# A two-layer attention kernel on one core: the stick-breaking scan as a running product, with a part of the splitting moved to GpSimd

## The chip, the core and the metric

The kernel runs on one core of a Trainium2 chip. The metric is the device time of one execution in microseconds (us). Three executions of the kernel before took 2713.68, 2715.38 and 2715.46 us; the median is 2715.38 us. One more execution was profiled.

## What is computed

The program is two layers for 2048 tokens of 1024 features, in float32. Layer 0 is a gated linear attention; the change does not touch it. Layer 1 is stick-breaking attention with 16 heads of 64 features:

```python
z = einsum('bhtd,bhsd->bhts', q_block, k) * scale
strictly_before = s_idx < t_idx
log_beta = log_sigmoid(z)
log_one_minus = where(strictly_before, log_beta - z, 0.0)
log_survive = cumsum(log_one_minus, axis=3, reverse=True) - log_one_minus
weights = where(strictly_before, exp(log_beta + log_survive), 0.0)
o = einsum('bhts,bhsd->bhtd', weights, v)
out = (o * silu(g)) @ w_out
```

A key s has beta = sigmoid(z); its weight is beta times the product of (1 - beta) of all keys between it and the query. Around it stand a modulated norm ahead and the output projection and a last norm behind.

## The kernel before, in words

**Layout.** Features lie on the partitions. A float32 operand of a large product is held as hi + lo, both float32r, and three products are accumulated (`mm3`, L150 to L152). The tokens come in 4 groups of 512 (g), layer 1's heads in 8 pairs (p).

**Layer 1.** For each pair and group, `pair_linear` makes keys, values, queries and gate of the group (L734 to L799). A `Unit` is a head (h) and a group of queries (g) against one group of keys (c); for a head it goes from c = g, the diagonal, down to c = 0. A unit has four tiles of 128 queries (tb), each 128x512, on the diagonal 128, 256, 384 and 512 wide. The work of a tile:

- `scores` (L815): two products make z in a bank of the pool `pz`, which has two banks (L821, L822). ScalarE makes S = sigmoid(z) in SBUF (L825) and 1 - beta = sigmoid(-z) in the bank itself (L826). On the diagonal GpSimd masks 128 columns of S (L828). VectorE scans from the last key back: S[s] = (1 - beta[s]) S[s + 1] + beta[s] (L830), started with 0 on the diagonal, elsewhere with the first column of the tile of the unit before. The bank is free when the scan is done.
- `turn` (L834): for 128 keys (sb), up to four transposes of S tiles into a bank pt of the pool `pw`, of two banks (L838); ScalarE copies it as sh (hi, L841), VectorE makes sl = pt - sh (lo, L842).
- `values` (L845): two products of sh and sl with the differences of neighbouring values v (L854, L855), summed in the bank o. After the last, `finish` adds the halves (L867, L868) and multiplies by the gate.

```python
        steps = [(u, j) for u in units for j in range(4)]
        for i, (u, j) in enumerate(steps):
            u.scores(j)
            turns.append((u, j))
            step(fill, (i + 0.7) / len(steps))
            if len(values) > LAG_V: ...   # values of an earlier tile
            step(fill, (i + 1) / len(steps))
            if len(turns) > LAG_T: ...    # turn of the tile five steps back
```

**What sets the order.** TensorE's order is the order of the program text: the loop above (L978 to L995). A group has 8 (g + 1) steps. Between the steps runs the fill: the 33 parts of `pair_linear` of the next group (three products each), and in groups 2 and 3 the weights of the next pair (`load_scaled`: splits L132, L133 and weighted sums L138, L140). In layer 1 the orders of ScalarE, VectorE, GpSimd and of the DMA queue on SP are made by a scheduler at build time and are then fixed: each engine takes its instructions in that order and waits by semaphores. `S`, `sh`, `sl` and others are tiles of one pool of 22 buffers (`m2`).

## Time and profile before

| | |
|---|---|
| median of three runs | 2715.38 us |
| profiled execution, first to last instruction | 2716.1 us |
| TensorE busy, matmuls | 2622.9 us (97%) |
| VectorE busy | 2112.2 us (78%) |
| ScalarE busy | 1785.9 us (66%) |
| GpSimd busy | 131.7 us (5%) |
| scans L830, 384 off the diagonal | 490.1 us |
| sl, L842, 640 | 381.3 us |
| second sigmoid L826, 640 | 344.4 us |

The profiled execution's own time is its span, 2716.1 us, 0.7 us over the median of the runs; the profile gives no other time around it. Layer 0 ends near 975 us, the attention of layer 1 runs from there to about 2600 us, and the last projection ends the program. The profile has the engines as PE (TensorE), PEld (its weight loads), ACT (ScalarE), DVE (VectorE), POOL (GpSimd) and SP. Matmuls overlap in the pipeline, so a busy PE is not one at its peak; the start-to-start distance of matmuls tells its pace.

### The profile page before, as it was taken

What the parts mean: (1) busy time and instruction counts of PE and PEld (TensorE: products, weight loads), DVE (VectorE), ACT (ScalarE), POOL (GpSimd) and SP (SyncE); (2) the same over time, 40 slices, a digit from 0 to 9 for tenths busy, and PEclk for the clock granted to TensorE, in tenths of its full rate; (3) what the DMA queues carried; (4) which work ended last, traced back from release to release, by engine and by line L of the source; (5) the groups of instructions that cost most, each with busy time, mean ns of one, the idle gap of its engine ahead of it and who ended that gap; (6) DMA issues with size and microseconds to landing.
All of it is one profiled execution on the core that took longest, in us unless ns stands there. A gap on an engine that the chain in (4) does not pass through costs nothing.

```text
span 2716.1 us, 38447 instructions
## 1 busy us (share of the span) xinstructions
PE 2622.9 (97%) x14040; PEld 2190.1 (81%) x14040; DVE 2112.2 (78%) x2933; ACT 1785.9 (66%) x3317; POOL 131.7 (5%) x358
## 2 busy tenths in 40 slices
PE   5999999999999999999999999999999999999998
PEld 4888888888788878788787887887887887877887
DVE  7657767676675658978979969979879789789866
ACT  4746756574584457767857857767768677677744
POOL 3000000000000010000000000000000000000000
PEclk7999999999999999999999999999999999999999
DMA  6326445545631563342343334243243243323464
GB/s 246 116 76 211 150 150 179 166 142 176 225 140 63 178 238 119 105 144 89 104 138 124 108 109 152 83 143 110 75 148 109 73 149 113 115 92 114 147 214 147
DMA packets 116685, 371.93 MB, mean 137 GB/s; under 512 B 13872, under 2 KB 18096, under 8 KB 116496
## 3 DMA queue, kind: packets, MB, share of 16 engines
q1 hardware_dynamic: 116496, 369.47, 40.8%
q8 instruction: 111, 1.82, 0.3%
q14 instruction: 78, 0.64, 0.1%
HBM read 311.75 MB, written 40.89 MB: 130 GB/s over the span
## 4 chain that ended last, share of the span: by engine, by line
PE 72%; DVE 17%; ACT 5%; DMA 3%; issue 3%; SPq 0%; POOL 0%; DVEq 0%; POOLq 0%
PE pt L838 6%; DVE S L830 5%; PE z L821 4%; PE z L822 3%; PE o L855 3%; PE o L854 3%; DVE sl L842 2%; PE pg L150 2%; PE pf L150 2%; PE pf L151 2%; PE pf L152 2%; PE pg L152 2%; PE pg L151 2%; PE lv L150 2%; PE pv L444 2%
## 5 line engine op out<-in xcount | busy, mean ns | idle before, releaser
L841 ACT ACTIVATE sh<-pt 128x512 fp32r<-128x512 f32 (+3 forms) x640 | 341.0, 533 | 318.1 <-PE pt L838 305.7
L830 DVE TENSOR_TENSOR_SCAN S<-z,S,S 128x512 f32<-128x512 f32 x384 | 490.1, 1276 | 33.0 <-ACT z L826 30.8
L842 DVE TENSOR_TENSOR sl<-pt,sh 128x512 fp32r<-128x512 f32 (+3 forms) x640 | 381.3, 596 | 141.1 <-ACT sh L841 137.6
L825 ACT ACTIVATE S<-z 128x512 f32<-128x512 f32 (+3 forms) x640 | 340.1, 531 | 24.4 <-PE z L822 12.3
L838 PE MATMUL pt<-ident,S 128*128 128x128 f32 x2176 | 343.3, 273 | 2.4 <-DVE sl L842 2.4
L826 ACT ACTIVATE z<-z 128x512 f32<-128x512 f32 (+3 forms) x640 | 344.4, 538 | 0.0
L838 PEld LDWEIGHTS pt<-ident,S 128*128 128x128 f32 x2176 | 270.3, 140 | 68.7 <-issue 2.7
L821 PE MATMUL z<-k,q 128*128 128x512 f32 (+3 forms) x640 | 287.2, 449 | 32.6 <-DVE S L830 30.2
L830 DVE TENSOR_TENSOR_SCAN S<-z,S 128x128 f32<-128x128 f32 (+3 forms) x256 | 209.5, 819 | 34.3 <-ACT z L826 24.2
L822 PE MATMUL z<-k,ql 128*128 128x512 f32 (+3 forms) x640 | 234.7, 367 | 0.9 <-DMA ql<-ql 0.9
L855 PE MATMUL o<-sl,v 128*128 128x512 f32 (+3 forms) x640 | 234.0, 366 | 0.0
L854 PE MATMUL o<-sh,v 128*128 128x512 f32 (+3 forms) x640 | 231.3, 361 | 0.6
L821 PEld LDWEIGHTS z<-k,q 128*128 128x128 f32 x640 | 121.4, 190 | 63.0 <-DVE S L830 56.2
L444 PE MATMUL pv<-wh_v,h 128*128 128x256 f32 x512 | 155.6, 304 | 0.0
L445 PE MATMUL pv<-wl_v,h 128*128 128x256 f32 x512 | 145.6, 284 | 0.0
L446 PE MATMUL pv<-wh_v,h 128*128 128x256 f32 x512 | 145.6, 284 | 0.0
L854 PEld LDWEIGHTS o<-sh,v 128*128 128x128 f32 x640 | 120.5, 188 | 30.2 <-DVE oB L868 3.7
L828 POOL TENSOR_SCALAR_AFFINE_SELECT S<-S 128x128 f32<-128x128 f32 x256 | 81.9, 320 | 1295.2 <-ACT S L825 1174.8
L855 PEld LDWEIGHTS o<-sl,v 128*128 128x128 f32 x640 | 120.5, 188 | 25.3
L822 PEld LDWEIGHTS z<-k,ql 128*128 128x128 f32 x640 | 123.1, 192 | 1.2 <-issue 1.0
L150 PE MATMUL pg<-h,wh_g 128*128 128x512 f32 x256 | 112.6, 440 | 0.0
L150 PE MATMUL lk<-xb,wh_w_kv 128*128 128x512 f32 x256 | 102.0, 398 | 5.2 <-DVE oB L868 5.2
(267 smaller groups left out, 6420.3 us busy)
## 6 DMA issues: line engine op xcount, KB each, us to landing
xb<-xn SPq DMA_DIRECT2D x256, 512.0 KB, 4.9
wa_l<-in_w_ada_dram SPq DMA_DIRECT2D x40, 512.0 KB, 6.0
wr_f<-in_w_out_dram SPq DMA_DIRECT2D x40, 512.0 KB, 4.0
x<-in_x_dram SPq DMA_DIRECT2D x32, 512.0 KB, 6.4
wr_v<-in_w_v_dram SPq DMA_DIRECT2D x32, 512.0 KB, 4.6
wr_kq<-in_w_kq_dram SPq DMA_DIRECT2D x32, 512.0 KB, 4.0
wr_g<-in_w_g_dram SPq DMA_DIRECT2D x32, 512.0 KB, 3.8
wr_out<-in_w_out_dram SPq DMA_DIRECT2D x32, 512.0 KB, 3.8
```

Of the source, the lines that this page charges most:

```text
L150: nc.tensor.matmul(out, hi, x[kt][0], start=first and i == 0, stop=False)
L444: nc.tensor.matmul(o, xh, hi, start=i == 0, stop=False)
L821: nc.tensor.matmul(z, L.q[:, h, tcol], k[:, h, 0:w], start=True, stop=False)
L822: nc.tensor.matmul(z, L.ql[h][:, tcol], k[:, h, 0:w], start=False, stop=True)
L825: nc.scalar.activation(s, z, AF.Sigmoid, scale=SCALE_B)
L826: nc.scalar.activation(z, z, AF.Sigmoid, scale=-SCALE_B)
L830: nc.vector.tensor_tensor_scan(s[:, ::-1], z[:, ::-1], s[:, ::-1], 0.0 if diag else self.before.S[tb][:, 0:1], ALU.mult, ALU.add)
L838: nc.tensor.transpose(pt[:, tb * P:(tb + 1) * P], self.S[tb][:, sb * P:(sb + 1) * P], ident)
L841: nc.scalar.activation(hi, pt[:, t0 * P:], AF.Copy)
L842: nc.vector.tensor_tensor(lo, pt[:, t0 * P:], hi.bitcast(F32), op=ALU.subtract)
L854: nc.tensor.matmul(o, v, hi, start=self.diag and sb == 0, stop=False)
L855: nc.tensor.matmul(o, v, lo, start=False, stop=self.c == 0 and sb == 3)
```

## The change

S is replaced by its complement, the running product of 1 - beta, so that one sigmoid is enough, and the transposed tile is brought back by -1 (which makes -S; the differences of the values change sign too).

- Off the diagonal one sigmoid, sigmoid(-z), is written into the bank; the scan reads the bank and a column of ones broadcast to 512 columns: min((1 - beta[s]) S[s + 1], 1).
- On the diagonal the one sigmoid goes to SBUF; the mask fills with 1; the scan reads that tile twice, in place.
- In `turn`, sh is a copy with bias -1. For odd sb off the diagonal ScalarE makes a second copy sf with the bias, and GpSimd makes sl = sf - sh from SBUF. In the others VectorE makes sl = (pt - 1) - sh.

```diff
-        nc.vector.tensor_tensor(dv[:, 1:], vt[:, 1:], vt[:, 0:TG - 1], op=ALU.subtract)
+        nc.vector.tensor_tensor(dv[:, 1:], vt[:, 0:TG - 1], vt[:, 1:], op=ALU.subtract)
...
-            nc.scalar.activation(s, z, AF.Sigmoid, scale=SCALE_B)
-            nc.scalar.activation(z, z, AF.Sigmoid, scale=-SCALE_B)
             if diag:
+                nc.scalar.activation(s, z, AF.Sigmoid, scale=-SCALE_B)
                 nc.gpsimd.affine_select(s[:, w - P:], s[:, w - P:], pattern=[[-1, P]],
-                                        compare_op=ALU.is_gt, fill=0.0, base=0, channel_multiplier=1)
-            nc.vector.tensor_tensor_scan(s[:, ::-1], z[:, ::-1], s[:, ::-1],
-                                       0.0 if diag else self.before.S[tb][:, 0:1], ALU.mult, ALU.add)
+                                        compare_op=ALU.is_gt, fill=1.0, base=0, channel_multiplier=1)
+                nc.vector.tensor_tensor_scan(s[:, ::-1], s[:, ::-1], s[:, ::-1], 1.0, ALU.mult, ALU.min)
+            else:
+                nc.scalar.activation(z, z, AF.Sigmoid, scale=-SCALE_B)
+                nc.vector.tensor_tensor_scan(s[:, ::-1], z[:, ::-1], ones.broadcast_to([P, TG]), self.before.S[tb][:, 0:1],
+                                           ALU.mult, ALU.min)
...
-            nc.scalar.activation(hi, pt[:, t0 * P:], AF.Copy)
-            nc.vector.tensor_tensor(lo, pt[:, t0 * P:], hi.bitcast(F32), op=ALU.subtract)
+            nc.scalar.activation(hi, pt[:, t0 * P:], AF.Copy, bias=-1.0)
+            if not self.diag and sb % 2:
+                full = t2(f"sf_{self.n}_{sb}")
+                nc.scalar.activation(full, pt, AF.Copy, bias=-1.0)
+                nc.gpsimd.tensor_tensor(lo, full, hi.bitcast(F32), op=ALU.subtract)
+            else:
+                nc.vector.scalar_tensor_tensor(lo, pt[:, t0 * P:], -1.0, hi.bitcast(F32),
+                                               op0=ALU.add, op1=ALU.subtract)
```

(The first column of dv changes its sign too; the other lines of the diff are comments.) TensorE's rows are the same in number and order. Three places show what moves; in the names S, z, pt, sh, sl and sf the numbers are pair, group of queries, head, group of keys and tile, and the last one counts tiles. A scan stands as SCALAR_TENSOR_TENSOR.

VectorE in pair 3, group 2, second head, from the third diagonal tile (S_3_2_1_2_2) to the first off the diagonal, before:

```order
L830 SCALAR_TENSOR_TENSOR S_3_2_1_2_2_15550<-z_3_2_1_2_2_15547,S_3_2_1_2_2_15550 128x384
L842 TENSOR_TENSOR sl_3_2_0_0_1_15569<-pt_3_2_0_0_1_15563,sh_3_2_0_0_1_15568 128x512
L140 SCALAR_TENSOR_TENSOR wacc_4_15195<-wr_w_kv4_0_15526,cond_kv_2178,wacc_4_15195 128x256
L133 SCALAR_TENSOR_TENSOR wl_w_qg4_0_15887<-wr_w_qg4_0_15884,a_l1_6032,wh_w_qg4_0_15886 128x256
L830 SCALAR_TENSOR_TENSOR S_3_2_1_2_3_15575<-z_3_2_1_2_3_15572,S_3_2_1_2_3_15575 128x512
L140 SCALAR_TENSOR_TENSOR wacc_4_15195<-wr_w_kv4_0_15526,cond_kv_2178,wacc_4_15195 128x256
L138 TENSOR_SCALAR wacc_4_15195<-wr_w_qg4_0_15884,cond_l1_4112 128x256
L842 TENSOR_TENSOR sl_3_2_0_0_2_15594<-pt_3_2_0_0_2_15588,sh_3_2_0_0_2_15593 128x512
L140 SCALAR_TENSOR_TENSOR wacc_4_15195<-wr_w_kv4_1_15690,cond_kv_2178,wacc_4_15195 128x256
L140 SCALAR_TENSOR_TENSOR wacc_4_15195<-wr_w_qg4_0_15884,cond_l1_4112,wacc_4_15195 128x256
L830 SCALAR_TENSOR_TENSOR S_3_2_1_1_0_15600<-z_3_2_1_1_0_15597,S_3_2_1_2_0_15490,S_3_2_1_1_0_15600 128x512
L842 TENSOR_TENSOR sl_3_2_0_0_3_15618<-pt_3_2_0_0_3_15612,sh_3_2_0_0_3_15617 128x512
```

and now:

```order
L831 SCALAR_TENSOR_TENSOR S_3_2_1_2_2_15664<-S_3_2_1_2_2_15664 128x384
L140 SCALAR_TENSOR_TENSOR wacc_4_15303<-wr_w_kv4_0_15640,cond_kv_2178,wacc_4_15303 128x256
L138 TENSOR_SCALAR wacc_4_15303<-wr_w_qg4_0_16003,cond_l1_4112 128x256
L140 SCALAR_TENSOR_TENSOR wacc_4_15303<-wr_w_kv4_1_15806,cond_kv_2178,wacc_4_15303 128x256
L140 SCALAR_TENSOR_TENSOR wacc_4_15303<-wr_w_qg4_0_16003,cond_l1_4112,wacc_4_15303 128x256
L831 SCALAR_TENSOR_TENSOR S_3_2_1_2_3_15692<-S_3_2_1_2_3_15692 128x512
L140 SCALAR_TENSOR_TENSOR wacc_4_15303<-wr_w_kv4_1_15806,cond_kv_2178,wacc_4_15303 128x256
L140 SCALAR_TENSOR_TENSOR wacc_4_15303<-wr_w_qg4_0_16003,cond_l1_4112,wacc_4_15303 128x256
L140 SCALAR_TENSOR_TENSOR wacc_4_15303<-wr_w_kv4_1_15806,cond_kv_2178,wacc_4_15303 128x256
L851 SCALAR_TENSOR_TENSOR sl_3_2_0_0_2_15712<-pt_3_2_0_0_2_15706,sh_3_2_0_0_2_15711 128x512
L834 SCALAR_TENSOR_TENSOR S_3_2_1_1_0_15718<-z_3_2_1_1_0_15715,S_3_2_1_2_0_15600,ones_93 128x512
L140 SCALAR_TENSOR_TENSOR wacc_4_15303<-wr_w_kv4_1_15806,cond_kv_2178,wacc_4_15303 128x256
```

The sl of tiles 1 and 3 are gone from VectorE, and weighted sums (L140) of the next pair's weights have moved up into their room.

GpSimd at the same place, before:

```order
L751 COPY vl_3_3_15356<-vt_3_3_15354 128x1
L757 TENSOR_TENSOR dv_3_3_15358<-vt_3_3_15354,vl_3_2_14876 128x1
L828 AFFINE_SELECT S_3_2_1_2_0_15490<-S_3_2_1_2_0_15490 128x128
L828 AFFINE_SELECT S_3_2_1_2_1_15518<-S_3_2_1_2_1_15518 128x128
L828 AFFINE_SELECT S_3_2_1_2_2_15550<-S_3_2_1_2_2_15550 128x128
L828 AFFINE_SELECT S_3_2_1_2_3_15575<-S_3_2_1_2_3_15575 128x128
```

and now:

```order
L849 TENSOR_TENSOR sl_3_2_0_1_1_15572<-sf_3_2_0_1_1_15574,sh_3_2_0_1_1_15571 128x512
L829 AFFINE_SELECT S_3_2_1_2_0_15600<-S_3_2_1_2_0_15600 128x128
L849 TENSOR_TENSOR sl_3_2_0_1_3_15623<-sf_3_2_0_1_3_15625,sh_3_2_0_1_3_15622 128x512
L829 AFFINE_SELECT S_3_2_1_2_1_15631<-S_3_2_1_2_1_15631 128x128
L829 AFFINE_SELECT S_3_2_1_2_2_15664<-S_3_2_1_2_2_15664 128x128
L849 TENSOR_TENSOR sl_3_2_0_0_1_15684<-sf_3_2_0_0_1_15686,sh_3_2_0_0_1_15683 128x512
L829 AFFINE_SELECT S_3_2_1_2_3_15692<-S_3_2_1_2_3_15692 128x128
L849 TENSOR_TENSOR sl_3_2_0_0_3_15735<-sf_3_2_0_0_3_15737,sh_3_2_0_0_3_15734 128x512
```

The masks of the diagonal tiles now stand between the low parts.

ScalarE at the same place, before:

```order
L841 ACTIVATE sh_3_2_0_0_1_15568<-pt_3_2_0_0_1_15563 128x512
L825 ACTIVATE S_3_2_1_2_3_15575<-z_3_2_1_2_3_15572 128x512
L826 ACTIVATE z_3_2_1_2_3_15572<-z_3_2_1_2_3_15572 128x512
L841 ACTIVATE sh_3_2_0_0_2_15593<-pt_3_2_0_0_2_15588 128x512
L825 ACTIVATE S_3_2_1_1_0_15600<-z_3_2_1_1_0_15597 128x512
L826 ACTIVATE z_3_2_1_1_0_15597<-z_3_2_1_1_0_15597 128x512
L841 ACTIVATE sh_3_2_0_0_3_15617<-pt_3_2_0_0_3_15612 128x512
```

and now:

```order
L845 ACTIVATE sh_3_2_0_0_1_15683<-pt_3_2_0_0_1_15678 128x512
L848 ACTIVATE sf_3_2_0_0_1_15686<-pt_3_2_0_0_1_15678 128x512
L828 ACTIVATE S_3_2_1_2_3_15692<-z_3_2_1_2_3_15689 128x512
L845 ACTIVATE sh_3_2_0_0_2_15711<-pt_3_2_0_0_2_15706 128x512
L833 ACTIVATE z_3_2_1_1_0_15715<-z_3_2_1_1_0_15715 128x512
L845 ACTIVATE sh_3_2_0_0_3_15734<-pt_3_2_0_0_3_15729 128x512
L848 ACTIVATE sf_3_2_0_0_3_15737<-pt_3_2_0_0_3_15729 128x512
```

The copy sf stands directly behind sh of the odd tiles, ahead of the next sigmoid.

## Rows read from the trace of the kernel before

**Rows 1.** The page, parts 1 and 4: busy time of each engine with its share of the span, and shares of the chain that ended last.
```profile
PE 2622.9 (97%) x14040; PEld 2190.1 (81%) x14040; DVE 2112.2 (78%) x2933; ACT 1785.9 (66%) x3317; POOL 131.7 (5%) x358
...
PE 72%; DVE 17%; ACT 5%; DMA 3%; issue 3%; SPq 0%; POOL 0%; DVEq 0%; POOLq 0%
```
**Rows 2.** Waits over the whole span: who waited for whom, us in total, times, longest.
```profile
ACT sh L841 <- PE pt L838: 305.7, 379, 2.9
...
PEld z L821 <- DVE S L830: 56.2, 99, 2.8
```
**Rows 3.** Timeline of TensorE in pair 2, group 3: start us, us, what.
```profile
1503.35 0.60 PE L838 MATMUL pt<-ident,S 128*128 128x128 f32 x4
1503.70 0.48 PE L821 MATMUL z<-k,q 128*128 128x512 f32 x1
...
1505.41 0.60 PE L838 MATMUL pt<-ident,S 128*128 128x128 f32 x4
```
**Rows 4.** The same at the end of pair 1's group 2 (in brackets: idle time before, and what ended it).
```profile
1302.27 0.62 PE L838 MATMUL pt<-ident,S 128*128 128x128 f32 x4
...
1303.20 0.19 PEld L821 LDWEIGHTS z<-k,q 128*128 128x128 f32 x1 [0.55 <-DVE S L830]
1303.20 0.33 PE L821 MATMUL z<-k,q 128*128 128x128 f32 x1 [0.31 <-DVE S L830]
```
**Rows 5.** Waits from 1000 to 2400 us.
```profile
PEld lk L150 <- DVE oB L868: 5.7, 7, 0.9
...
PEld o L854 <- DVE oB L868: 3.7, 7, 0.5
```
**Rows 6.** Busy time by stretch, groups 0 to 3 of pair 3: from:to, length, then the busy us (and instructions) of PE, PEld, DVE, ACT and POOL in this order, granted clock, DMA share, GB/s.
```profile
1564.00:1595.90 31.90, 31.90 (x164) 26.57 (x162) 17.71 (x25) 14.91 (x32) 2.67 (x10) 1.00 0.25 73
1595.90:1635.50 39.60, 39.60 (x214) 33.24 (x211) 31.88 (x43) 26.95 (x57) 2.67 (x10) 1.00 0.48 163
1635.50:1691.90 56.40, 53.32 (x280) 42.88 (x277) 53.38 (x84) 44.92 (x96) 2.85 (x10) 1.00 0.37 123
1691.90:1758.10 66.20, 64.97 (x353) 53.59 (x353) 63.74 (x86) 53.55 (x110) 2.91 (x10) 1.00 0.31 98
```
**Rows 7.** Waits from 1635.5 to 1691.9 us: pair 3, group 2.
```profile
PEld z L821 <- DVE S L830: 4.8, 8, 1.4
```
**Rows 8.** Waits from 1691.9 to 1758.1 us: pair 3, group 3.
```profile
PEld z L821 <- DVE S L830: 1.8, 5, 0.5
```
**Rows 9.** Timeline of TensorE's weight loads in pair 3, group 2: the loads of z in the run of waits.
```profile
1672.54 0.19 PEld L821 LDWEIGHTS z<-k,q 128*128 128x128 f32 x1 [0.41 <-DVE S L830]
1675.77 0.19 PEld L821 LDWEIGHTS z<-k,q 128*128 128x128 f32 x1 [1.14 <-DVE S L830]
...
1681.66 0.19 PEld L821 LDWEIGHTS z<-k,q 128*128 128x128 f32 x1 [1.36 <-DVE S L830]
1684.09 0.19 PEld L821 LDWEIGHTS z<-k,q 128*128 128x128 f32 x1 [0.79 <-DVE S L830]
```
**Rows 10.** Busy time in the stretch of that run, columns as in rows 6.
```profile
1672.50:1684.30 11.80, 9.29 (x42) 6.99 (x43) 11.73 (x19) 8.00 (x16) 0.00 (x0) 1.00 0.67 190
```
**Rows 11.** Groups of instructions by line and form, whole span: count | busy us, mean ns of one | idle before, releasers.
```profile
L830 DVE TENSOR_TENSOR_SCAN S<-z,S,S 128x512 f32<-128x512 f32 x384 | 490.1, 1276 | 33.0 <-ACT z L826 30.8
...
L842 DVE TENSOR_TENSOR sl<-pt,sh 128x512 fp32r<-128x512 f32 x448 | 302.1, 674 | 130.9 <-ACT sh L841 129.2 <-issue 0.4 <-PE pt L838 0.2
...
L826 ACT ACTIVATE z<-z 128x512 f32<-128x512 f32 x448 | 270.0, 603 | 0.0
L841 ACT ACTIVATE sh<-pt 128x512 fp32r<-128x512 f32 x448 | 267.5, 597 | 249.6 <-PE pt L838 245.6 <-DVE ss_f L204 2.0 <-PE o L854 0.8
...
L830 DVE TENSOR_TENSOR_SCAN S<-z,S 128x512 f32<-128x512 f32 x64 | 78.2, 1221 | 23.0 <-ACT z L826 22.5 <-POOL S L828 0.6
```
**Rows 12.** The same of ScalarE: an activation whose bias is a column.
```profile
L798 ACT ACTIVATE g<-lg,wbias 128x512 f32<-128x512 f32 x32 | 21.9, 684 | 2.7 <-PE lg L152 1.6
```
**Rows 13.** The same of VectorE: the weight operations, a scan with both inputs in SBUF (e), and operations with one input in a bank (pk, pq).
```profile
L133 DVE SCALAR_TENSOR_TENSOR wl_w_qg<-wr_w_qg,a_l,wh_w_qg 128x256 fp32r<-128x256 f32 x64 | 29.1, 471 | 2.3 <-ACT wh_w_qg L132 2.3
...
L408 DVE TENSOR_TENSOR_SCAN e<-masks,gk 128x512 f32<-128x512 bf16 x16 | 19.5, 1218 | 0.2
...
L457 DVE TENSOR_TENSOR gk<-pk,gk 128x512 f32<-128x512 f32 x16 | 11.0, 684 | 8.4 <-PE pk L152 8.4
L464 DVE SCALAR_TENSOR_TENSOR e<-pq,e 128x512 f32<-128x512 f32 x16 | 10.9, 683 | 2.3 <-PE pq L152 2.3
```
**Rows 14.** Single lines: duration in ns, least/median/most; first and last start in us; forms. L323 and L244 run side by side from 21.3 to 38.3 us.
```profile
L323 POOL TENSOR_TENSOR x<-x,r_x x8: 1713/2242/2244, 21.3 to 36.1; 128x512 f32<-128x512 f32 x8
...
L244 DVE SCALAR_TENSOR_TENSOR aa_l<-wa_l,s_col,aa_l x35: 1273/1284/2174, 13.2 to 728.8; 128x1024 f32<-128x1024 f32 x35
...
L828 POOL TENSOR_SCALAR_AFFINE_SELECT S<-S x256: 287/292/1656, 979.4 to 2525.3; 128x128 f32<-128x128 f32 x128
```
**Rows 15.** Timeline in pair 3, groups 2 and 3: sh of an odd tile on ScalarE, and the product with its sl.
```profile
1702.71 0.60 ACT L841 ACTIVATE sh<-pt 128x512 fp32r<-128x512 f32 x1
...
1707.23 0.40 PE L855 MATMUL o<-sl,v 128*128 128x512 f32 x1
```
**Rows 16.** Timeline in pair 1, group 3: a scan on VectorE and a mask on GpSimd.
```profile
1304.06 1.26 DVE L830 TENSOR_TENSOR_SCAN S<-z,S,S 128x512 f32<-128x512 f32 x1
...
1304.08 0.29 POOL L828 TENSOR_SCALAR_AFFINE_SELECT S<-S 128x128 f32<-128x128 f32 x1 [23.51 <-ACT S L825]
```

More of the change, by code (lines that the diff above doesn't have):

```diff
@@ L752, in pair_linear @@
         dv = t2(f"dv_{n}")
-        nc.vector.tensor_tensor(dv[:, 1:], vt[:, 1:], vt[:, 0:TG - 1], op=ALU.subtract)
+        nc.vector.tensor_tensor(dv[:, 1:], vt[:, 0:TG - 1], vt[:, 1:], op=ALU.subtract)
         if prev is None:
-            nc.gpsimd.tensor_copy(dv[:, 0:1], vt[:, 0:1])
+            nc.gpsimd.tensor_scalar(dv[:, 0:1], vt[:, 0:1], -1.0, None, op0=ALU.mult)
         else:
-            nc.gpsimd.tensor_tensor(dv[:, 0:1], vt[:, 0:1], prev.last, op=ALU.subtract)
+            nc.gpsimd.tensor_tensor(dv[:, 0:1], prev.last, vt[:, 0:1], op=ALU.subtract)
         pk = bank(pl, f"lk_{n}")
```

## The prediction

> **What bounds the kernel now.** I read the page first. TensorE is busy 97% of the span and holds 72% of the chain that ended last; VectorE holds 17% of that chain [rows 1]. So the change, which touches no TensorE instruction (its 13246 rows stand in the same order before and after), can only shorten the time by waits of TensorE. Which waits those are is in the table of waits: before the weights of a score tile z are loaded (L821) TensorE stands 56.2 us in 99 waits, for the scan L830 that still reads the bank [rows 2]. A timeline shows that these are lost in full. In an undisturbed stretch of pair 2 a step repeats after 2.06 us, and z starts 0.35 us after its transposes; in a disturbed step of pair 1 it starts 0.93 us after them, 0.58 us late, and the weight load shows 0.55 us of waiting there, the matmul only 0.31 [rows 3, 4]. I count weight-load waits. From 1000 to 2400 us a second kind shows: 5.7 and 3.7 us in which a bank is freed late by L868 [rows 5]. Together 65.6 us: the most that the change can give by waits.
>
> Where they lie: pair 3 stands for pairs 1 to 6. Its groups 0 and 1 run at TensorE's pace (31.9 and 39.6 us, TensorE busy throughout, VectorE 17.7 and 31.9). Group 2 takes 56.4 us with VectorE busy 53.4, group 3 66.2 us with VectorE 63.7 [rows 6]; their z waits are 4.8 and 1.8 us [rows 7, 8]. In group 2 most of it is one run of four waits (0.41, 1.14, 1.36, 0.79: 3.7 us) [rows 9], and in that run VectorE is busy 11.73 of 11.80 us while TensorE has 9.29 us of work [rows 10]. So z waits because VectorE is behind, and VectorE is behind because of its own queue. ScalarE is not it: its copy L841 waits 305.7 us for the transposes [rows 2].
>
> **The change, part by part.**
> The sigmoid L826 goes: 344.4 us of ScalarE in 640 pieces, 0.60 us at full width [rows 11]. ScalarE waits for TensorE, so none of this is on the path by itself. It is worth two things: the scan can start one sigmoid (0.60 us) earlier after its z, and a diagonal tile's bank is free after the sigmoid alone, no longer after mask and scan.
> The copy sf comes: 192 pieces (off the diagonal, odd sb: per pair 4, 8 and 12 in groups 1 to 3) of 0.60 us, as L841 [rows 11]: 115 us of ScalarE, hidden in the 344 just freed. It stands right behind sh on ScalarE, so in odd steps the next sigmoid waits 0.60 us longer and the two shifts cancel; in even steps 0.60 us is kept.
> Bias -1 in sh and sf: no row has it. Bounds: 0 and 0.087 us a piece (0.684 for an activation with a bias column against 0.597 without [rows 11, 12]); the nearest form, a copy with constants, is the lower one. I take 0; at the upper bound 832 x 0.087 = 72 us lie on ScalarE, hidden too.
> The low part: in the remaining tiles tensor_tensor becomes scalar_tensor_tensor. Same shape, one input in a bank: 0.684 us for the one, 0.683 for the other [rows 13]: 0.
> The scan off the diagonal reads the constant 1 in place of S, with min for add. No row has a broadcast input. The full-width scans of three kinds of inputs take 1.276, 1.221 and 1.218 us [rows 11, 13], so bounds of -0.06 and +0.06 us, and I take 0 as it is nearest to the first. The diagonal scan now has both inputs in SBUF, as the 1.218 has: 0. The sign of dv and the mask's fill: same instructions, 0.
> The 192 odd low parts leave VectorE: 0.674 us each [rows 11], per pair 2.7, 5.4 and 8.1 us in groups 1 to 3. This is the term that matters. GpSimd takes them; its full-width two-input form took 2.24 us in the only place that shows it, beside a busy VectorE [rows 14], so 192 x 2.24 = 430 us on an engine that is busy 132 us [rows 1].
> What GpSimd holds up: the diagonal masks now queue behind a low part. But a mask no longer holds a bank, and its S is turned five steps later. Who waits for GpSimd: L855's successor, the product with the low part. From the end of sh to that product, one of the tightest odd tiles has 3.92 us (1703.31 to 1707.23) [rows 15]; sf and the low part need 0.60 + 2.24. I take 0. SP's order changes only by neighbours that swap.
>
> **What VectorE pays back.** With low parts on GpSimd, two engines read SBUF side by side. The trace has one such place: while GpSimd did eight two-input operations, the two-input operation L244 of VectorE took 2.17 us in place of 1.28 [rows 14]. With one input in a bank nothing is seen: a scan beside a mask keeps 1.26 us [rows 16]. So a low part on GpSimd can hold a VectorE operation with two SBUF inputs by up to 0.89 us, and L830 off the diagonal or L842 by nothing. The Trainium skill ("SBUF — State Buffer", Who interferes with whom) says that a Vector instruction with two SBUF inputs and a GpSimd instruction that reads SBUF exclude each other for a whole instruction. The rows agree for L244; by that rule alone every such meeting costs, which is the second rival below.
> Such operations on VectorE in groups 2 and 3 are the weight splits L133, the sums L140, and now the diagonal scans. In group 2 they stand close together just where the run of waits is: the piece of VectorE's order that the part on the change shows has two diagonal scans and eight weight operations in twelve rows, and GpSimd's piece has three low parts among the masks of the same four tiles. I charge half the price, 0.45 us a low part, because a meeting can fall anywhere in the operation.
>
> **The sum, per pair.** Group 3: 8.1 us off VectorE, 12 x 0.45 = 5.4 back, for 1.8 us of waits: all 1.8 go. Group 2: the waits outside the run (4.8 - 3.7 = 1.1) go. Ahead of and in the run four odd low parts leave (2.7) and the earlier scan gives 0.60 once, 4 x 0.45 = 1.8 come back: 1.5 of the run's 3.7 go. So 4.4 of 6.6 us a pair, 7 x 4.4 = 30.8. Start and last pair have the other 56.2 - 46.2 = 10.0 us of z waits; two thirds go as well, 6.7. Of the 9.4 us for L868, whose queue on VectorE is shorter, I take half: 4.7. Sum 42.2 us: 2716.1 - 42.2 = 2673.9. The profiled execution is 0.7 us over the median of the runs, so **2673 us**.
>
> **The rivals.**
> *All waits go* (VectorE gets far enough ahead, as GpSimd's reads fall between): 65.6 us, 2650. For it: VectorE has 5.4 and 8.1 us less to do than before against waits of 4.8 and 1.8. Against: the run in group 2 is local. Chance 0.20.
> *Full price on the shared reads*: every low part holds one VectorE operation for 0.89 us. Group 3 then gets 12 x 0.89 = 10.7 back for 8.1, group 2's run 3.6 for 3.3, and only group 2's scattered 1.1 us and a third of the start's and end's 10.0 go: 7 x 1.1 + 3.3 = 11 us, 2704. For it: in rows 14 nearly every one of GpSimd's eight operations met one of VectorE's. Against: most of VectorE's time in group 3 is scans and low parts with one input in a bank. Chance 0.12.
> *Nothing reaches TensorE*, as the moved weight operations fill VectorE's free time at the same place: 2715. Chance 0.04.
> *GpSimd late, slower than before*: in place of the scan TensorE waits for the low part at its product. Place: the 160 odd tiles of groups 2 and 3. Decides from: 3.92 - 0.60 = 3.3 us for a low part, queueing included. A mask on GpSimd has taken 1.66 us where 0.29 is usual [rows 14], so stretching happens. If a low part needed 4.2 us, 0.9 x 160 = 144 us come in and 42 go: 2715.4 + 144 - 42 = 2817. Against: 2.24 us was already under full opposition. Chance 0.04.
>
> **How the numbers follow.** The forecast itself has 0.60. Its own range is 2664 to 2690: at a quarter of the 0.89 us the run in group 2 gives 2.4 and a pair 5.3 us, with start and end some 50 in all; at three quarters the run gives 0.6, group 3 half of its 1.8, a pair 2.6, in all some 26. The range reaches from all waits gone, 2650, to near full price, 2700, and leaves out about 0.15. A measurement of this kernel tells 0.2% (5.4 us) from no change: faster has the forecast, the first rival and nearly all of the second, 0.91; same 0.05; slower 0.04.
>
> **What would show it.** Right: weight-load waits of z for the scan near 19 us instead of 56; in pair 3 group 2 near 53.8 us (56.4 - 2.6) and group 3 near 64.4 (66.2 - 1.8); VectorE's scans still 1.28 us; the weight operations L133 in part longer than their 0.47 us [rows 13]. Wrong: scans off the diagonal over 1.34 us; weight loads of the low product waiting for GpSimd for over 5 us in sum; or weight operations at their old lengths, which would make the first rival right.

## The result, and the profile after

The changed kernel takes 2742.93 us (median of 4 runs, 2742.42 to 2745.53) against 2714.53 us before: a ratio of 1.0107 with a 95% interval of 1.0092 to 1.0121. It is slower by 28 us where 42 us of gain were forecast. The profiled execution has a span of 2740.9 us.

The page, parts 1 and 4, of the change (the lines that answer to [rows 1]):

```profile
PE 2628.7 (96%) x14040; PEld 2200.7 (80%) x14040; DVE 2032.0 (74%) x2741; ACT 1608.6 (59%) x2869; POOL 407.5 (15%) x550
...
PE 71%; DVE 18%; issue 5%; ACT 4%; DMA 1%; POOL 0%; SPq 0%; DVEq 0%; POOLq 0%; ACTq 0%
```

VectorE and ScalarE have less to do, as intended (2032.0 and 1608.6 us against 2112.2 and 1785.9), and yet VectorE's share of the chain rose from 17 to 18%. The waits over the whole span of the change (us in total, times, longest), beside [rows 2]:

```profile
DVE S L831 <- POOL S L829: 167.2, 90, 4.2
...
PEld pt L842 <- DVE sl L851: 42.1, 35, 3.1
...
PEld z L821 <- DVE S L834: 20.0, 32, 2.4
```

The row that the prediction looked at did what was forecast: 56.2 us became 20.0 (near 19 was said). But a new one stands beside it: the transposes into pt wait 42.1 us for a bank that VectorE's low part L851 still reads. In the same view of the kernel before, that wait was 1.3 us:

```profile
PEld pt L838 <- DVE sl L842: 1.3, 2, 1.0
```

And not all of the wait for the scan is gone from the loads of z; some of it has another name. Their idle time of all kinds (the sum behind the last bar) was 63.0 us before and is 44.3 us in the change:

```profile
L821 PEld LDWEIGHTS z<-k,q 128*128 128x128 f32 x640 | 121.4, 190 | 63.0 <-DVE S L830 56.2 <-ACT x1n L230 0.8 <-issue 0.2
...
L821 PEld LDWEIGHTS z<-k,q 128*128 128x128 f32 x640 | 122.6, 192 | 44.3 <-DVE S L834 20.0 <-ACT sh L845 11.1 <-issue 6.8
```

TensorE's 14040 instructions are the same in both traces, so their start-to-start distances can be subtracted one by one. Over layer 1: ahead of transposes +38.9 us, ahead of z -16.6, distances that grew by 0.1 to 0.3 us with no wait +11.5 (mostly the lower clock, below), the rest -8.8. The sum is +25.0 us, the whole difference of the spans (24.8).

Busy time by stretch, groups 2 and 3 of pair 3 and then of pair 4 (columns as in [rows 6]):

```profile
1643.30:1701.00 57.70, 53.62 (x281) 43.77 (x279) 53.08 (x79) 37.54 (x78) 11.28 (x17) 0.97 0.35 119
1701.00:1770.80 69.80, 66.66 (x354) 54.83 (x353) 56.99 (x71) 45.89 (x91) 20.36 (x23) 0.98 0.30 92
...
1842.20:1899.90 57.70, 52.44 (x281) 42.74 (x279) 53.06 (x79) 37.52 (x78) 11.27 (x17) 1.00 0.35 119
1899.90:1968.20 68.30, 65.17 (x356) 53.61 (x353) 56.95 (x71) 45.74 (x91) 20.43 (x23) 1.00 0.31 94
```

Groups 0 and 1 keep their 31.9 and 39.6 us. Group 2 takes 57.7 us (56.4 before) although it has five instructions fewer on VectorE: VectorE is still busy 53.1 us. So its instructions became longer. The groups of instructions from 977 to 2600 us show which (count | busy us, mean ns):

```profile
L834 DVE TENSOR_TENSOR_SCAN S<-z,S,ones 128x512 f32<-128x512 f32 x384 | 486.1, 1274 | 40.4 <-ACT z L833 33.8 <-POOL sl L849 4.0 <-PE o L865 1.0
...
L849 POOL TENSOR_TENSOR sl<-sf,sh 128x512 fp32r<-128x512 f32 x190 | 253.9, 1337 | 740.7 <-ACT sf L848 432.4 <-PE lg L152 127.8 <-PE lk L152 101.1
...
L133 DVE SCALAR_TENSOR_TENSOR wl_w_qg<-wr_w_qg,a_l,wh_w_qg 128x256 fp32r<-128x256 f32 x56 | 38.3, 713 | 0.2
...
L140 DVE SCALAR_TENSOR_TENSOR wacc<-wr_w_kv,cond_kv,wacc 128x256 f32<-128x256 f32 x49 | 31.7, 646 | 0.0
...
L133 DVE SCALAR_TENSOR_TENSOR wl_w_kv<-wr_w_kv,a_kv,wh_w_kv 128x256 fp32r<-128x256 f32 x52 | 28.4, 576 | 0.0
...
L140 DVE SCALAR_TENSOR_TENSOR wacc<-wr_w_qg,cond_l,wacc 128x256 f32<-128x256 f32 x49 | 23.3, 476 | 0.7
```

The scan with one input in a bank keeps 1.274 us (1.276 before). The splits and weighted sums, with two inputs in SBUF and 0.47 us each before, now have means up to 0.71: the four rows above take 121.7 us together, where the same four took 95.7, so 26 us of stretching. Two of the four in the kernel before:

```profile
L133 DVE SCALAR_TENSOR_TENSOR wl_w_kv<-wr_w_kv,a_kv,wh_w_kv 128x256 fp32r<-128x256 f32 x52 | 23.8, 468 | 0.0
...
L140 DVE SCALAR_TENSOR_TENSOR wacc<-wr_w_kv,cond_kv,wacc 128x256 f32<-128x256 f32 x49 | 23.0, 470 | 0.0
```

The largest of the new waits is at the place that the three order listings of the change show: pair 3, group 2, second head. The timelines there, first VectorE, then GpSimd, ScalarE and TensorE:

```profile
1677.68 1.04 DVE L831 TENSOR_TENSOR_SCAN S<-S 128x384 f32<-128x384 f32 x1
1678.65 0.45 DVE L140 SCALAR_TENSOR_TENSOR wacc<-wr_w_kv,cond_kv,wacc 128x256 f32<-128x256 f32 x1
1679.02 0.34 DVE L138 TENSOR_SCALAR wacc<-wr_w_qg,cond_l 128x256 f32<-128x256 f32 x1
1679.29 0.47 DVE L140 SCALAR_TENSOR_TENSOR wacc<-wr_w_kv,cond_kv,wacc 128x256 f32<-128x256 f32 x1
1679.68 0.47 DVE L140 SCALAR_TENSOR_TENSOR wacc<-wr_w_qg,cond_l,wacc 128x256 f32<-128x256 f32 x1
1680.08 1.21 DVE L831 TENSOR_TENSOR_SCAN S<-S 128x512 f32<-128x512 f32 x1
1681.22 1.42 DVE L140 SCALAR_TENSOR_TENSOR wacc<-wr_w_kv,cond_kv,wacc 128x256 f32<-128x256 f32 x1
1682.56 0.47 DVE L140 SCALAR_TENSOR_TENSOR wacc<-wr_w_qg,cond_l,wacc 128x256 f32<-128x256 f32 x1
1682.95 0.48 DVE L140 SCALAR_TENSOR_TENSOR wacc<-wr_w_kv,cond_kv,wacc 128x256 f32<-128x256 f32 x1
1683.35 0.68 DVE L851 SCALAR_TENSOR_TENSOR sl<-pt,sh 128x512 fp32r<-128x512 f32 x1
```

```profile
1681.09 1.27 POOL L849 TENSOR_TENSOR sl<-sf,sh 128x512 fp32r<-128x512 f32 x1 [3.17 <-issue]
...
1677.86 0.60 ACT L845 ACTIVATE sh<-pt 128x512 fp32r<-128x512 f32 x1 [1.35 <-PE pt L842]
...
1681.06 0.40 PE L865 MATMUL o<-sl,v 128*128 128x512 f32 x1
1684.09 1.10 PE L842 MATMUL pt<-ident,S 128*128 128x128 f32 x4 [2.63 <-DVE sl L851]
```

The low part of tile 2 had all its inputs when sh ended, at 1678.46, and started at 1683.35, 4.9 us later, behind a scan and seven weight operations that the scheduler had put ahead of it; in the order before, a scan and four stood between it and the low part of tile 1. One of them met GpSimd's low part and took 1.42 us in place of 0.47. Both causes are in these rows: the queue ahead of it (some 3.9 of the 4.9 us) and the meeting (0.95). TensorE waited 2.63 us for the bank.

In group 3 the copy of the next pair's bias (L727) now stands behind a scan. VectorE, then TensorE:

```profile
1752.25 1.27 DVE L834 TENSOR_TENSOR_SCAN S<-z,S,ones 128x512 f32<-128x512 f32 x1
1753.44 0.12 DVE L727 COPY wbias<-pb 128x2 f32<-128x2 f32 x1
1755.58 0.75 DVE L778 SCALAR_TENSOR_TENSOR ql<-lq,wbias,q 64x512 fp32r<-64x512 f32 x1 [2.02 <-ACT q L777]
1756.36 0.76 DVE L780 SCALAR_TENSOR_TENSOR ql<-lq,wbias,q 64x512 fp32r<-64x512 f32 x1
1757.15 0.29 DVE L851 SCALAR_TENSOR_TENSOR sl<-pt,sh 128x128 fp32r<-128x128 f32 x1
...
1757.49 0.66 PE L842 MATMUL pt<-ident,S 128*128 128x128 f32 x4 [1.10 <-DVE sl L851]
```

ScalarE needs the bias for q, VectorE stands 2.02 us for q at the head of its queue, and a low part waits behind it.

### The profile page after: what moved, and what is told of

Same layout as the page of the kernel before. It is cut to its first block, busy times and chain, and to the rows that moved or that the text cites. A ratio compares the mean times of both kernels' runs of the same rounds, so it can differ in the third digit from the quotient of the medians.

```text
span 2740.9 us, 38707 instructions
## 1 busy us (share of the span) xinstructions
PE 2628.7 (96%) x14040; PEld 2200.7 (80%) x14040; DVE 2032.0 (74%) x2741; ACT 1608.6 (59%) x2869; POOL 407.5 (15%) x550
## 4 chain that ended last, share of the span: by engine, by line
PE 71%; DVE 18%; issue 5%; ACT 4%; DMA 1%; POOL 0%; SPq 0%; DVEq 0%; POOLq 0%; ACTq 0%
PE pt L842 6%; DVE S L834 6%; PE z L821 3%; PE z L822 3%; PE o L865 3%; PE o L864 3%; PE pg L150 2%; PE pg L152 2%; PE pg L151 2%; PE pf L150 2%; PE pf L151 2%; PE pf L152 2%; DVE sl L851 2%; PE pv L444 2%; PE py L150 2%
## 5 line engine op out<-in xcount | busy, mean ns | idle before, releaser
L834 DVE TENSOR_TENSOR_SCAN S<-z,S,ones 128x512 f32<-128x512 f32 x384 | 486.1, 1274 | 40.4 <-ACT z L833 33.8
L842 PE MATMUL pt<-ident,S 128*128 128x128 f32 x2176 | 348.5, 276 | 32.2 <-DVE sl L851 32.2
L849 POOL TENSOR_TENSOR sl<-sf,sh 128x512 fp32r<-128x512 f32 x192 | 257.0, 1338 | 759.9 <-ACT sf L848 451.6
L842 PEld LDWEIGHTS pt<-ident,S 128*128 128x128 f32 x2176 | 270.8, 142 | 107.6 <-DVE sl L851 42.1
L831 DVE TENSOR_TENSOR_SCAN S<-S 128x128 f32<-128x128 f32 (+3 forms) x256 | 212.5, 833 | 171.4 <-POOL S L829 167.2
L821 PE MATMUL z<-k,q 128*128 128x512 f32 (+3 forms) x640 | 286.8, 448 | 25.6 <-DVE S L834 24.7
L851 DVE SCALAR_TENSOR_TENSOR sl<-pt,sh 128x512 fp32r<-128x512 f32 (+1 forms) x448 | 253.0, 566 | 77.0 <-ACT sh L845 72.4
L833 ACT ACTIVATE z<-z 128x512 f32<-128x512 f32 x384 | 226.9, 591 | 92.9 <-PE z L822 76.5
L821 PEld LDWEIGHTS z<-k,q 128*128 128x128 f32 x640 | 122.6, 192 | 44.3 <-DVE S L834 20.0
L829 POOL TENSOR_SCALAR_AFFINE_SELECT S<-S 128x128 f32<-128x128 f32 x256 | 93.1, 366 | 424.9 <-ACT S L828 407.5
L482 POOL TENSOR_SCALAR_AFFINE_SELECT sc<-sc 128x512 f32<-128x512 f32 x16 | 11.9, 746 | 816.7 <-ACT sc L480 696.2
L848 ACT ACTIVATE sf<-pt 128x512 f32<-128x512 f32 x192 | 114.1, 594 | 1.0 <-PE o L864 0.8
```

Source lines behind the costliest of these rows:

```text
L821: nc.tensor.matmul(z, L.q[:, h, tcol], k[:, h, 0:w], start=True, stop=False)
L831: nc.vector.tensor_tensor_scan(s[:, ::-1], s[:, ::-1], s[:, ::-1], 1.0, ALU.mult, ALU.min)
L833: nc.scalar.activation(z, z, AF.Sigmoid, scale=-SCALE_B)
L834: nc.vector.tensor_tensor_scan(s[:, ::-1], z[:, ::-1], ones.broadcast_to([P, TG]), self.before.S[tb][:, 0:1], ALU.mult, ALU.min)
L842: nc.tensor.transpose(pt[:, tb * P:(tb + 1) * P], self.S[tb][:, sb * P:(sb + 1) * P], ident)
L849: nc.gpsimd.tensor_tensor(lo, full, hi.bitcast(F32), op=ALU.subtract)
```

## The experiments

Two theories stood at the start. **Order**: the loss comes from where the weight operations and the bias copy now stand on VectorE. **Shared reads**: it comes from VectorE's two-input operations being held while GpSimd reads. A third, the **scan theory**: it comes from the scan part itself. Ratios are against the kernel before on the same chip, with their 95% intervals.

**scan_only**: one sigmoid and the running product, all low parts on VectorE.

```diff
-            if not self.diag and sb % 2:
-                full = t2(f"sf_{self.n}_{sb}")
-                ...
-            else:
-                nc.vector.scalar_tensor_tensor(lo, ...)
+            nc.vector.scalar_tensor_tensor(lo, ...)
```

> The change with all low parts on VectorE: no copy sf, nothing on GpSimd but the masks. Order theory (the loss comes from where the weighted sums, the bias copy and the low parts now stand on VectorE): the bias copy of the next pair still stands behind a scan in group 3 (1.25 + 0.34 us a pair, some 11 us), but the sums are packed less (at most four in a row ahead of a low part), so between 2695 and 2712. Shared-read theory (the loss comes from VectorE's two-input weight operations being held up by GpSimd): no operation is held, L133 and L140 at 0.47 us, and the gain of the early scan shows in full, 2685 to 2700. Scan theory (the loss comes from the one-sigmoid scan itself): slower than 2715, as in the change, 2730 to 2743.

Measured 2723.97 us, 1.0041 (1.0028 to 1.0053), above the ranges of the first two theories and below that of the third: a loss with no low part on GpSimd, and about a third of the change's. TensorE's transposes wait 20.5 us for low parts (2.4 before); the bias copy stands behind the scan here too.

**low_only**: the kernel before, with sf and GpSimd's low parts.

```diff
-            nc.vector.tensor_tensor(lo, pt[:, t0 * P:], hi.bitcast(F32), op=ALU.subtract)
+            if not self.diag and sb % 2:
+                full = t2(f"sf_{self.n}_{sb}")
+                nc.scalar.activation(full, pt, AF.Copy)
+                nc.gpsimd.tensor_tensor(lo, full, hi.bitcast(F32), op=ALU.subtract)
+            else:
+                ...
```

> The kernel before with its two sigmoids and its scan; only the odd low parts off the diagonal go to GpSimd, by a second copy. Order theory: the sums are packed ahead of the low part in group 2 as in the change, but the bias copy stands ahead of the scan, so the loss of group 2 without that of group 3: 2722 to 2735. Shared-read theory: L133 and L140 as long as in the change, 26 us in all, and a loss of about the same size: 2730 to 2743. Scan theory: no loss, 2700 to 2715.

Measured 2747.08 us, 1.0114 (1.0098 to 1.0130), above both ranges: the whole loss of the change, and more, without its scan. TensorE's z waits rise to 61.5 us (30.2 before, by the matmul).

**moves**: in the change, four rows of each pair but the last stand earlier in VectorE's order: three low parts in group 2 and the bias copy in group 3. The order is held by a table; each instruction gets an edge that orders it behind the one ahead, with no wait.

```diff
+    for a, b in zip(place, place[1:]):      # place: VectorE's instructions in the wished order
+        tc.add_manual_dep(mine[b], mine[a].name,
+                          ...
+                          reason="held order")
```

> The change, with the order of VectorE held except at four places of each pair but the last: in group 2 three low parts stand two to six rows earlier, ahead of the weighted sums; in group 3 the bias copy stands ahead of the scan again. Nothing is left out. Order theory: TensorE's waits for a low part before its transposes (2.8, 0.8 and 1.25 us a pair over the kernel before) go, 7 x 4.9 = 34 us: 2709, and less if the waits of z behind them go as well. Shared-read theory: the stretched operations keep VectorE behind and the wait moves to the next scan: 2725 to 2740.

Measured 2721.81 us, 1.0027 (1.0018 to 1.0037), between the two ranges: 21 of the 28 us are gone. TensorE's waits by the matmul, in the kernel before, the change and this run:

```profile
PE z L821 <- DVE S L830: 30.2, 50, 2.4
```

```profile
PE pt L842 <- DVE sl L851: 32.2, 21, 2.7
PE z L821 <- DVE S L834: 24.7, 43, 2.2
```

```profile
PE z L821 <- DVE S L834: 38.0, 49, 2.2
...
PE pt L842 <- DVE sl L851: 4.3, 4, 2.2
```

The waits for low parts fell from 32.2 us to 4.3, as the order theory said, and 13 us came back as waits for the scan (24.7 to 38.0), as the other theory said.

**no_read**: the change, VectorE's and ScalarE's orders held, and no subtraction on GpSimd.

```diff
-                nc.gpsimd.tensor_tensor(lo, full, hi.bitcast(F32), op=ALU.subtract)
+                nc.gpsimd.memset(lo.bitcast(F32), 0.0)
```

> The change with VectorE's and ScalarE's orders held as they are, and a memset on GpSimd in place of the low part (the subtraction is left out): GpSimd reads nothing from SBUF there and waits for no copy. Order theory: L133 and L140 fall back to 0.47 us, but the low part of group 2 still stands behind seven sums and the bias copy behind its scan: 1.3 of the 2.8 us stay, and all of the 1.25: 2720 to 2732. Shared-read theory: 26 us of stretching go, and the waits with them: 2705 to 2717.

Measured 2721.07 us, 1.0018 (1.0008 to 1.0028), at the lower end of the order theory's range and above the other's: in the same order on VectorE and ScalarE most of the loss goes as well, while 19.0 us of waits for low parts stay. So either change alone, four rows moved or no subtraction, gives back some 21 of the 28 us. The two cannot be added, and neither makes the forecast gain.

**scan_border** and **after_border**: the scan part and the whole change, with VectorE's order of the kernel before (save for ql, and in after_border the low parts that GpSimd makes).

> The scan part alone (as scan_only), with VectorE's order held as in the kernel before, except that in each pair a product's low half (ql) stands behind a scan off the diagonal that was ahead of it in the program text. Order theory: the waits of TensorE's transposes for a low part (23.7 us more than before in layer 1 of scan_only) go and the z waits stay less than before: 2695 to 2705. Rival, the scan part itself costs (the scan with a broadcast input, the bank held by one sigmoid): 2715 to 2724 as in scan_only.

> The whole change with VectorE's order held as in the kernel before, odd low parts left out of it, and the same exception for ql. Order theory: the waits for low parts go (39 us over the kernel before in layer 1), what GpSimd's reads stretch (26 us) falls into VectorE's freed time: 2695 to 2712. Shared-read theory: stretched weight operations stand directly ahead of low parts and scans and keep TensorE waiting: 2715 to 2730.

scan_border: 2718.68 us, 1.0011 (1.0002 to 1.0020), in the rival's range; the gain that the order theory expected was missed. The waits for low parts are gone, and the scan part gains nothing:

```profile
PE z L821 <- DVE S L834: 31.9, 35, 1.7
...
PE pt L842 <- DVE sl L846: 3.3, 4, 2.7
```

after_border: 2731.42 us, 1.0060 (1.0039 to 1.0082). The order theory's expectation, a gain, was missed here too, and the time is just above the other's range: the order of before takes back 12 of the 28 us and no more.

**text_scan** and **text_after**: the same two with VectorE in the order of the program text up to the last pair's group 1.

> The scan part alone, with VectorE's instructions of layer 1 up to the last pair's group 1 in the order of the program text: in each step the scan, that step's share of the weights, the low part of five steps back. Order theory: no low part stands behind more than one step's weights: 2690 to 2705. Rival, a fixed order behind the products makes VectorE wait for TensorE and ScalarE and gives the time back: 2712 to 2730.

> The whole change, with VectorE's instructions of layer 1 up to the last pair's group 1 in the order of the program text. Order theory: as text_scan with the odd low parts off VectorE: 2690 to 2708. Shared-read theory: the stretched operations, one a step, still delay the scan or the low part behind them by up to 0.95 us each: 2712 to 2730.

text_scan: 2724.98 us, 1.0042 (1.0027 to 1.0056), in the rival's range. text_after: 2759.94 us, 1.0168 (1.0152 to 1.0184), far above both ranges. Text order is no cure, and with both in the order of the text GpSimd's low parts cost 35 us.

**border_set** and **border_copy**: after_border with ScalarE's order held too, and GpSimd's subtraction replaced as in no_read, or by `nc.gpsimd.tensor_copy(lo, full)`.

> As after_border (VectorE's order as before; ScalarE's held as it is there), with a memset on GpSimd in place of the low part (the subtraction is left out): nothing is read there and no copy waited for. Shared-read theory: L133 and L140 back at 0.47 us and most of the 16 us over the kernel before go: 2700 to 2716. Rival, what is left there comes from the buffers and the second copy on ScalarE that the low part brings: 2725 to 2732 as after_border.

> As border_set, with a copy of sf on GpSimd in place of the low part (the subtraction is left out): one operand is read instead of two, and the copy is waited for. If any read of GpSimd holds VectorE's two-input operations: L133 and L140 stretched as in after_border, 2722 to 2732. If only a two-input operation of GpSimd does: as border_set, 2700 to 2716.

border_set: 2693.30 us, 0.9930 (0.9915 to 0.9945), below both ranges. border_copy: 2699.10 us, 0.9949 (0.9934 to 0.9964), just below the range for the case that only a two-input operation of GpSimd holds VectorE. Here is a gain, about half of the forecast 42 us: in the order of before and without the subtraction the change would be 20 us faster. With no_read, after_border and the change this makes a table (us). VectorE and ScalarE have the same order within each row; between the rows ScalarE's differs too:

| | with the subtraction | memset in its place |
|---|---|---|
| orders of the change | 2742.93 (the change) | 2721.07 (no_read) |
| VectorE's order of before | 2731.42 (after_border) | 2693.30 (border_set) |

The subtraction costs 38 us in the order of before and 22 in that of the change; the change's orders cost 28 us without the subtraction and 12 with it. Each alone is enough to turn the gain into a loss, and they overlap. One line of GpSimd and the most stretched split, of after_border, border_copy and border_set:

```profile
L849 POOL TENSOR_TENSOR sl<-sf,sh 128x512 fp32r<-128x512 f32 x191 | 249.6, 1307 | 754.3 <-ACT sf L848 557.0 <-PE lk L152 88.2 <-issue 67.2
L133 DVE SCALAR_TENSOR_TENSOR wl_w_kv<-wr_w_kv,a_kv,wh_w_kv 128x256 fp32r<-128x256 f32 x52 | 35.2, 688 | 0.0
```

```profile
L849 POOL CAST sl<-sf 128x512 fp32r<-128x512 f32 x192 | 121.7, 634 | 808.7 <-ACT sf L848 587.2 <-PE lk L152 92.7 <-issue 78.5
...
L133 DVE SCALAR_TENSOR_TENSOR wl_w_kv<-wr_w_kv,a_kv,wh_w_kv 128x256 fp32r<-128x256 f32 x52 | 27.3, 535 | 0.8 <-ACT wh_w_kv L132 0.8
```

```profile
L849 POOL MEMSET sl<- 128x512 f32 x192 | 100.8, 525 | 498.5 <-PE o L864 125.5 <-PE pd L792 122.1 <-PE o L865 86.4
...
L133 DVE SCALAR_TENSOR_TENSOR wl_w_kv<-wr_w_kv,a_kv,wh_w_kv 128x256 fp32r<-128x256 f32 x52 | 23.9, 470 | 3.3 <-ACT wh_w_kv L132 3.3
```

The split goes from 0.688 to 0.535 to 0.470 us. The copy reads one operand, but is also half as long, so the runs do not tell the number of reads from their duration. The memset, besides, waits for no copy, and the masks behind it come sooner: VectorE waits for masks for 165.7 us in after_border and 119.2 in border_set. That the late masks make the loss is unlikely: in group 2 of pair 3 these waits are 3.0 and 2.4 us (3.3 and 1.7 in group 3), while the group takes 57.2 and 54.4:

```profile
1638.10:1695.30 57.20, 53.85 (x280) 43.99 (x279) 51.75 (x76) 37.85 (x78) 11.40 (x17) 0.97 0.35 116
```

```profile
1621.70:1676.10 54.40, 51.78 (x280) 42.95 (x278) 49.23 (x76) 37.72 (x78) 6.28 (x17) 1.00 0.36 121
```

Nor does any wait of TensorE name GpSimd, in either run or in the change.

**early_before** and **early_after**: half of the next pair's first weights (four splits, four sums) beside group 1 instead of group 2, in the kernel before and in the change.

```diff
+                if g == 1 and p + 1 < SBP:
+                    Ws[p + 1] = new_weights(p + 1)
+                    kv = pair_weights(p + 1, Ws[p + 1], 0)
+                    fill.append([kv, KT // 2, 0, 1, 0])
                 if g == 2 and p + 1 < SBP:
-                    Ws[p + 1] = new_weights(p + 1)
-                    fill.append([pair_weights(p + 1, Ws[p + 1], 0), KT, 0.5, 1, 0])
+                    fill.append([kv, KT // 2, 0.5, 1, 0])
...
```

> The kernel before, with the first half of the next pair's first weights (four splits, four sums on VectorE) made beside group 1 instead of group 2. TensorE's order is the same. If TensorE's z waits in group 2 come from VectorE's backlog there: 8 x 0.47 = 3.8 us less to do for 4.0 us of waits a pair, some 3 of them go: 2690 to 2702. Rival, they come from the scan's own chain: 2710 to 2716.

> The change with the same edit. Order and shared-read theories alike: fewer weights ahead of low parts and beside GpSimd's reads in group 2, where 2.8 and 0.8 us a pair are lost: 2712 to 2730. Rival, the loss does not come from the weights: 2738 to 2745.

early_before: 2692.71 us, 0.9927 (0.9912 to 0.9943), in the range of VectorE's backlog. early_after: 2701.54 us, 0.9955 (0.9939 to 0.9972), below both ranges: the loss comes from the weights more than either theory said. Groups 1 and 2 of pair 3 in early_before:

```profile
1579.60:1620.60 41.00, 40.57 (x213) 33.33 (x210) 37.01 (x59) 27.16 (x57) 3.18 (x10) 1.00 0.50 167
1620.60:1672.30 51.70, 51.59 (x281) 42.84 (x279) 48.54 (x71) 43.67 (x94) 2.68 (x10) 1.00 0.39 138
```

Group 2 runs at TensorE's pace, 51.7 us instead of 56.4, for 1.4 more in group 1. That VectorE's backlog in group 2 holds TensorE is thereby shown.

**free_border**: after_border with GpSimd's low parts only where VectorE makes no weights. **low_border**: low_only in VectorE's order of before.

```diff
-            if not self.diag and sb % 2:
+            if not self.diag and sb % 2 and free(self.g, self.h, self.c):
...
+    def free(g, h, c):
...
+        return g == 1 or g == 3 and h == 1
```

> The change, with GpSimd's low parts only in the turns beside which VectorE makes no weights (group 1, and the second head of group 3: 80 of the 192); the others are made by VectorE, and VectorE's order is that of the kernel before, as in after_border. Shared-read theory: L133 and L140 back near 0.47 us, the 16 us of after_border go, and what is left is scan_border (2718) less what group 3's second head saves: 2706 to 2718. Rival, GpSimd's low parts cost by the copy on ScalarE, the buffers or the masks behind them: 2720 to 2730.

> The low parts alone on GpSimd (as low_only, with the two sigmoids), VectorE's order held as in the kernel before. Shared-read theory: the reads cost here what they cost in after_border over scan_border, 12 us or more, since the scan also starts a sigmoid later: 2728 to 2745. Order theory: most of low_only's loss goes: 2712 to 2725.

free_border: 2720.01 us, 1.0019 (1.0009 to 1.0030), where the rival's range begins and 2 us above the shared reads'; low_border: 2737.47 us, 1.0085 (1.0070 to 1.0101), in the range of the shared reads: in the order of before the low parts alone lose 23 us. The 80 low parts of free_border that meet no weights cost nothing against scan_border (2718.68), and gain nothing; with the whole computation in place, the copies, buffers and late masks that these bring are free: VectorE waits 134.0 us for masks there and 15.5 us in scan_border. The other 112 cost after_border, net of the work that they take off VectorE, its 11 to 13 us over these two.

**early_scan** and **early_free**: the early weights, with the scan part, and with free_border's rule in the scheduler's own order.

> The scan part alone, with half of the next pair's first weights made beside group 1 (as early_before). If the scan part is worth nothing by itself, as early_before: 2688 to 2697. If the sigmoid saved shows once VectorE is not behind: 2675 to 2688. If the scheduler's order costs again as in scan_only: 2697 to 2706.

> The change with both edits: half of the first weights beside group 1, and GpSimd's low parts only in group 1 and the second head of group 3 (some weights stand beside group 1 now). Shared-read theory: better than early_after (2701), 2680 to 2697. Rival, the low parts cost by something else: 2697 to 2710.

early_scan: 2695.06 us, 0.9924 (0.9906 to 0.9942), as the case of a scan part that is worth nothing has it. early_free: 2693.05 us, 0.9924 (0.9908 to 0.9940), in the first range. Both are the same as early_before, so neither part of the change adds anything to it. early_before beats both kernels with eight fewer weight operations in group 2 and not a line of the change.

## Why the prediction was wrong, point by point

- **The bound** was read rightly. VectorE is behind in the run of group 2 [rows 9, 10], and early_before brings that group to TensorE's pace by moving 3.8 us of VectorE's work (an estimate: eight operations of 0.47 us). ScalarE is not it: of the sigmoid's 344 us nothing reached the time in scan_border.
- **The step that failed** is the one in the sum for group 2: low parts leave, and so VectorE is ahead by 2.7 us, and 0.6 for the earlier scan, less what the meetings give back. It took VectorE's order as given. The rows in the section on the change already showed sums moved up into the room of the low parts; the prediction named that only as a rival in which nothing reaches TensorE (2715), and never asked which low part stands behind the moved rows and who waits for its bank. Transposes that had waited 1.3 us waited 42.1. Undoing four such rows is worth 21 us (moves); the orders cost 12 us with the subtraction and 28 without. Group 2 of pair 3 took 57.7 us where 53.8 was the sign of being right, and group 3 took 69.8 where 64.4 was.
- **The shared reads** were the right mechanism, mis-sized in what they cost. Charged were 0.45 us for each of 16 low parts in groups 2 and 3, 7.2 us a pair; measured are 26 us of stretching over 7 pairs, 3.7 a pair. The charge was too high and the effect taken from it too low: a stretched operation does not only shorten a margin, it stands in a queue whose next instruction TensorE waits for. In after_border against border_set, 23.6 us of stretching (119.4 against 95.8 in the four rows of L133 and L140) go with 38 us of time, of which part is the clock (below). The Trainium skill ("SBUF — State Buffer", Who interferes with whom) has such meetings exclude each other for a whole instruction; the 1.42 us of L140 beside a 1.27 us low part agree, and so does the scan with its input in a bank, at 1.274 us.
- **The gain** was too large even with both left out: border_set gains 20 us, where the prediction had 42 with the reads charged and up to 65.6 without. Its own row for z came out in size (19 forecast, 20.0 measured), but partly by a change of name: the loads of z lost 18.7 us of idle time in all, not 36, since 11.1 us of waits now name ScalarE and 6.8 have no cause in the profile.
- **Right in size**: the scan with the broadcast ones (1.274 us); GpSimd's low part, 1.34 us under the bound of 2.24; bias -1 at nothing (sh 0.598 us, 0.597 before). GpSimd was not late for TensorE, though VectorE waits 167.2 us for masks.
- **The rival on the slower side** (GpSimd late, 2817) had the wrong mechanism. The rival of full price on the reads (2704) had the right mechanism and ended 39 us short of the change; even in the order of before the reads turn the gain into a loss of 16 us, where that rival still had a gain.
- **Left open**: why the scheduler packs the sums as it does was not tried; nor was the wait for two operands told from the length of the operation (border_copy).

## What to carry to other kernels

Work taken off a busy engine can move the order of what a scheduler places there. Read, at the place where the critical engine waits, which instruction now stands ahead of the one that it waits for, and price that queue; the sum of busy time says nothing of it. An engine that helps by reading the same memory belongs where its neighbour's two-input operations are not: there, 80 low parts on GpSimd cost nothing here (free_border), though they gained nothing either. And where one stretch is short of an engine, first look for work in that stretch that can move to another one.

## What the runs showed of the hardware

A wait of TensorE can cost more than its length, since the clock can fall behind it. In the change the same wait, 3.03 to 3.05 us from the start of the last product to that of the transposes, stands in group 2 of every pair but the last. Behind it the granted clock was 0.50 (1.2 GHz) in pair 2, and 1.00 (2.4 GHz) in pair 4 (columns as in [rows 6]):

```profile
1488.00:1492.00 4.00, 4.00 (x10) 3.13 (x11) 3.93 (x8) 1.04 (x2) 0.00 (x0) 0.50 0.66 201
...
1881.00:1887.00 6.00, 3.45 (x18) 2.73 (x19) 5.96 (x10) 1.83 (x3) 0.29 (x1) 1.00 0.22 70
```

It fell in pairs 0, 2, 3, 5 and 6 and not in 1 and 4. At the lower clock a 512-column product takes 0.43 us from start to start instead of 0.23; 8 to 10 products were caught in pairs 0, 3 and 6, some 1.6 to 2 us, and 18 in pairs 2 and 5, up to 3.6 us (estimates, from these two distances). In the kernel before, the run of four waits of up to 1.36 us [rows 9] brought no such fall: the clock stayed at 1.00 there [rows 10]. Yet in the change it fell to 0.50 in group 3 of pairs 3 and 5 behind shorter waits, of 1.10 and 1.09 us, so the length of a wait does not tell by itself.

The clock is a good part of what the reads cost. The profile of after_border has a mean granted clock of 0.981, that of border_set 0.990. Subtracting their distances one by one, layer 1 of after_border is 41.8 us longer: 10.7 ahead of transposes, 15.4 ahead of z, and 16.1 at 86 other products that met the lower clock in after_border alone, the rest -0.4. The lower clock is not needed for a loss, though: low_only loses 33 us at 0.989, where the profile before has 0.989 too.
